# Mixers head by head over both token halves, with the residual stream in DRAM and the output product behind the loop

## The chip, the cores and the metric

The kernel runs on one core of one Trainium2 chip. The metric is the device time of one execution in microseconds (us). Engines are named as in the profile: PE is TensorE (PEld its weight loads), DVE is VectorE, ACT is ScalarE, POOL is GpSimd, SP is SyncE, which here only issues DMAs.

## The reference

The input is x with 1024 tokens of 1024 numbers in float32. Two layers follow each other: layer 0 mixes tokens by gated linear attention (GLA, 4 heads, keys of 128, values of 256), layer 1 by the gated delta rule (GDN, 8 key heads and 16 value heads of 128, with a causal convolution of width 4 in front). Each is followed by a dense feed-forward part (FFN), and a norm ends the whole.

```python
for i in range(DEPTH):
    hn = rms_norm(h, mix_norm_w[i])
    if i % N_MIXERS == 0:
        h = h + gla_mixer(hn, ...)
    else:
        h = h + gdn_mixer(hn, ...)
    h = h + swiglu(rms_norm(h, ffn_norm_w[i]), ffn_w_gate_up[i], ffn_w_down[i])
return rms_norm(h, final_norm_w)
```

Both mixers have the same frame: a projection `hn @ w_in` gives q, k, v, gates and an output gate; a recurrence over the tokens keeps a state per head; its output is normed, multiplied by the SiLU of the output gate, and multiplied by `w_out`, which mixes all heads. The recurrence is computed by chunks of 128 tokens. For GDN each chunk needs the inverse of a triangular matrix (`solve` and `join` in the kernel).

## The kernel before, in words

**Precision.** Operands are split into a high and a low part, and a product takes three matmuls: high x high, low x high, high x low (`mm3`, L151 to L155; these three lines carry nearly all of PE's work). The high part of a weight block is an ACT cast (L122), the low part a POOL subtraction (L123), both in `loadw`, 128x1024 at a time.

**Tokens in halves.** The 1024 tokens are worked on in two halves of 512 columns. The residual stream `h` stays in SBUF all the time (4 MB, `self.h`). A mixer runs through units (half, head): 8 units in GLA, 16 in GDN (a GDN unit is one key head with its two value heads), all heads of half 0 first. So each unit loads and splits its head's weight blocks for its own half only, and each weight block is loaded and split twice in a layer. The states of all heads wait in SBUF (`S_`) for the second half.

**The order.** `pipeline` (L454) writes the steps of several units among each other by a string, in GLA

```python
"seq out-1 decay+1 late+1 prep+1 keys+2 post values+2",
```

and in GDN "solve+1 seq late+1 keys+2 out-1 prep+2 values+2 post join+1". `keys`, `values` and `late` are projections, `prep` builds the matrices of a unit's chunks, `solve` inverts 32x32 blocks on DVE (31 pairs L712, L714 that depend on each other), sends them through DRAM and back (L719, L722), `join` (L729 to L750) joins the blocks, `seq` is the recurrence chunk by chunk, `post` norms and gates its output. A scheduler then orders each engine's instructions; each engine runs its own queue in order.

**Output product.** `gateout` (L258) gates a unit's output and splits it (`ohi`, `olo`, L265, L266). `outproj` (L254) loads the 256 rows of `w_out` that belong to the unit, and `addout` (L231) adds their product to the residual, one DVE addition (L240) for each 128 tokens and 512 columns. This is the step `out-1`: the out-projection of the unit before, inside the loop.

**FFN.** `ffnhead` (L845) norms half 0 and does the first products of the FFN with it; it is the `tail` of the pipeline and stands within the last unit. `inputsums` (L910), at the FFN's start, needs the normed half 1 (L936, L940). The FFN's products use a scheme of seven block products instead of eight; `downs` (L1017) takes its down projection in passes of three or two k-tiles of each half of the rows, reads the activations (`act`) from DRAM, sums blocks (L1045), splits them (L1050, L1051) and adds each product to the residual (L1061).

## Time and profile before

| | before |
|---|---|
| median of 3 runs (lowest to highest) | 3312.35 us (3310.05 to 3316.11) |
| the profiled execution's own time | 3317.64 us |
| its span in the trace | 3315.9 us |
| mean granted clock of PE | 0.958 of full speed |
| busy: PE / DVE / ACT / POOL | 2979.9 / 2174.2 / 1386.2 / 1564.2 us |

In this execution the GLA mixer lasts to about 604 us, FFN 0 to 1283.5, the GDN mixer to about 2626, FFN 1 to about 3300; the final norm ends the span. The shares of busy time are means over these stages. A row of a timeline gives start, duration, engine, line, operation, tiles written and read, and in brackets how long the engine was idle before and what it waited for; x2 means two instructions in one row. Durations of PE overlap, so the rate of matmuls is read from their starts.

### The profile page before, as it was taken

The page shows a single profiled execution, that of the slowest core. Times are in us where ns is not written, and L with a number is a line of the kernel's source. Part 1 is how long each engine was busy: PE and PEld are TensorE (multiplying, and loading weights), DVE is VectorE, ACT ScalarE, POOL GpSimd, SP SyncE. Part 2 cuts the span into 40 slices and gives each one's busy share as a digit, 9 for nine tenths or more (in the row PEclk, how much of TensorE's full clock was granted, in tenths as well). Part 3 has the DMA queues.
Part 4 walks back from the last instruction along what each step waited for, and adds up shares of the span by engine and source line. Part 5 has one row for each costly group of instructions (what it writes and reads, how often), then busy time and mean ns, then how long its engine had stood idle before and what let it go on. Part 6 is the DMA issues. An engine that isn't in the chain of part 4 may idle for free. (4 is left out here: it accounts for less than half of the span.)

```text
span 3315.9 us, 40871 instructions
## 1 busy us (share of the span) xinstructions
PE 2979.9 (90%) x14323; PEld 2422.4 (73%) x14323; DVE 2174.2 (66%) x4493; ACT 1386.2 (42%) x2605; POOL 1564.2 (47%) x1069
## 2 busy tenths in 40 slices
PE   6988989799998999788898988899988889999898
PEld 5877877578886777677676766777776678887676
DVE  6465665633225996768888888888878542232998
ACT  5345444334343334444444544444444433333333
POOL 4344443455556874433333333333432355554885
PEclk9999999899999999899999999999999999999999
DMA  4222212322223312222222222222222232222331
GB/s 127 73 59 58 70 58 78 107 83 83 83 77 121 111 67 53 69 61 59 62 69 63 53 74 63 65 76 68 63 68 60 70 111 81 85 83 82 138 104 58
DMA packets 364924, 256.40 MB, mean 77 GB/s; under 512 B 67847, under 2 KB 309966, under 8 KB 364718
## 3 DMA queue, kind: packets, MB, share of 16 engines
q1 hardware_dynamic: 364654, 253.77, 25.8%
q8 instruction: 113, 1.85, 0.2%
q14 instruction: 93, 0.76, 0.1%
q0 software_dynamic: 64, 0.02, 0.0%
HBM read 219.12 MB, written 34.60 MB: 77 GB/s over the span
## 5 line engine op out<-in xcount | busy, mean ns | idle before, releaser
L123 POOL TENSOR_TENSOR wlo<-raw,whi 128x1024 fp32r<-128x1024 f32 x204 | 490.2, 2405 | 842.7 <-ACT whi L122 716.9
L153 PE MATMUL pd<-xhi,whi 128*128 128x512 f32 x1072 | 442.8, 414 | 0.9 <-ACT xhi L193 0.9
L154 PE MATMUL pd<-xlo,whi 128*128 128x512 f32 x1072 | 437.1, 408 | 0.0
L155 PE MATMUL pd<-xhi,wlo 128*128 128x512 f32 x1072 | 434.0, 405 | 0.0
L122 ACT CAST whi<-raw 128x1024 fp32r<-128x1024 f32 x204 | 214.0, 1049 | 295.0 <-issue 119.2
L895 POOL TENSOR_TENSOR olo<-s,ohi 128x512 fp32r<-128x512 f32 x152 | 195.9, 1290 | 206.1 <-ACT ohi L894 206.1
L895 POOL TENSOR_TENSOR olo<-raw,ohi 128x512 fp32r<-128x512 f32 x138 | 190.3, 1382 | 209.3 <-ACT ohi L894 181.7
L155 PEld LDWEIGHTS pd<-xhi,wlo 128*128 128x128 f32 x1072 | 205.6, 192 | 39.6 <-issue 0.3
L153 PEld LDWEIGHTS pd<-xhi,whi 128*128 128x128 f32 x1072 | 206.2, 193 | 38.7 <-ACT xhi L193 1.4
L154 PEld LDWEIGHTS pd<-xlo,whi 128*128 128x128 f32 x1072 | 206.6, 193 | 37.1
L153 PE MATMUL pd<-whi,ohi 128*128 128x512 f32 x384 | 164.5, 429 | 35.5 <-ACT k L586 22.5
L712 DVE TENSOR_TENSOR tmpx<-nbx,xix 128x60 f32<-128x60 f32 (+24 forms) x496 | 187.1, 377 | 9.9
L894 ACT CAST ohi<-s 128x512 fp32r<-128x512 f32 x152 | 94.3, 622 | 230.9 <-PE pd L154 172.9
L894 ACT CAST ohi<-raw 128x512 fp32r<-128x512 f32 x138 | 85.1, 621 | 197.9 <-POOL olo L895 176.0
L714 DVE TENSOR_TENSOR xix<-xix,tmpx 128x60 f32<-128x60 f32 (+24 forms) x496 | 160.9, 324 | 10.2
L154 PE MATMUL pd<-wlo,ohi 128*128 128x512 f32 x384 | 161.0, 419 | 0.0
L1051 POOL TENSOR_TENSOR blo<-t,bhi 128x1536 fp32r<-128x1536 f32 (+1 forms) x32 | 126.8, 3963 | 69.1 <-ACT bhi L1050 64.2
L155 PE MATMUL pd<-whi,olo 128*128 128x512 f32 x384 | 158.3, 413 | 0.9 <-DVE olo L266 0.9
L240 DVE TENSOR_TENSOR h<-h,pd 128x512 f32<-128x512 f32 x192 | 130.2, 682 | 44.0 <-PE pd L155 42.9
L1003 DVE TENSOR_TENSOR p<-p,pp 128x512 f32<-128x512 f32 x38 | 26.1, 688 | 197.5 <-DMA raw<-in_ffn_w_gate_up_dram 148.3
L153 PE MATMUL pd<-bhi,ahi 128*128 128x512 f32 x264 | 110.6, 419 | 36.7 <-DVE h L1061 21.3
L153 PEld LDWEIGHTS pd<-whi,ohi 128*128 128x128 f32 x384 | 76.0, 198 | 63.6 <-ACT k L586 27.2
(387 smaller groups left out, 8320.2 us busy)
## 6 DMA issues: line engine op xcount, KB each, us to landing
raw<-in_gdn_w_in_dram SPq DMA_DIRECT2D x96, 512.0 KB, 4.0
raw<-in_ffn_w_gate_up_dram SPq DMA_DIRECT2D x176, 256.0 KB, 3.3
raw<-in_gla_w_in_dram SPq DMA_DIRECT2D x48, 512.0 KB, 3.9
ra<-act SPq DMA_DIRECT2D x88, 256.0 KB, 5.1
rb<-in_ffn_w_down_dram SPq DMA_DIRECT2D x24, 768.0 KB, 6.5
raw<-in_gdn_w_out_dram SPq DMA_DIRECT2D x32, 512.0 KB, 4.2
act<-p SPq DMA_DIRECT2D x44, 256.0 KB, 2.0
act<-u SPq DMA_DIRECT2D x38, 256.0 KB, 2.0
```

The source lines that it names most:

```text
L122: nc.scalar.copy(hi, raw)
L123: nc.gpsimd.tensor_tensor(out=lo, in0=raw, in1=hi.bitcast(F32), op=ALU.subtract)
L153: mm(ps, lhs[0], rhs[0], start=first, stop=False, **kw)
L154: mm(ps, lhs[0], rhs[1], start=False, stop=False, **kw)
L155: mm(ps, lhs[1], rhs[0], start=False, stop=last, **kw)
L240: self.nc.vector.tensor_tensor(out=o, in0=o, in1=ps, op=ALU.add)
L712: V.tensor_tensor(out=tv, in0=nbx[:, s, s + 1:].unsqueeze(2).to_broadcast([P, n, w]), in1=xv[:, s:s + 1, 0:w].to_broadcast([P, n, w]), op= ...
L714: V.tensor_tensor(out=xv[:, s + 1:, 0:w], in0=xv[:, s + 1:, 0:w], in1=tv, op=ALU.add)
L894: self.nc.scalar.copy(hi, src)
L895: eng.tensor_tensor(out=lo, in0=src, in1=hi.bitcast(F32), op=ALU.subtract)
L1003: V.tensor_tensor(out=p1, in0=p1, in1=pb, op=ALU.add)
L1051: eng.tensor_tensor(out=lo, in0=src, in1=hi.bitcast(F32), op=ALU.subtract)
```

## The change

**Heads outside, halves inside.** `project` loads a weight block once and yields the product of both halves; the loops go over heads, and a head's state lives only through its two halves (a half of a head is called a half-step below). Each mixer block is so loaded and split once: the program's 128x1024 weight splits fall from 204 to 84 on ACT and on POOL, in GDN from eight to three in a half-step. The buffers of split weights go from three to two. The order is written out as calls in place of `pipeline` and its strings. Both halves are normed before the loop.

**The residual leaves SBUF.** `openh` loads it into a pool on the right side, `closeh` frees that pool behind the norms, and behind the mixer's loop it is loaded again, from x in layer 0 and from a DRAM copy (`spill`) in layer 1.

**The output product.** `gateout` only gates; the result goes to DRAM tiles `act`. Behind the loop `outs` does a direct product with the first four of these tiles, and `downs` takes the rest (four tiles in GLA, twelve in GDN) by the seven-product scheme, two k-tiles a pass (`most`). `ffnhead` follows.

```diff
-        self.h = self.cp.tile([P, KT, D], F32, name="h")
...
+        self.openh(a["x"][0])
...
+    def closeh(self):
+        self.hs.__exit__(None, None, None)
+
+    def weightpools(self, es):
+        self.wr, self.ws, self.tp = (self.pool(es, *x) for x in (("wraw", 2), ("wsplit", 2), ("units", 2)))
+
+    def mixer(self, stage, l, src, w_out):
+
+        with ExitStack() as es:
+            self.xp = self.pool(es, "xmix", 1)
+            self.weightpools(es)
+            act = stage(es)
+        self.openh(src)
...
+        with ExitStack() as es:
+            self.weightpools(es)
+            self.outs(w_out, act[:4])
+            self.downs(w_out[4 * P:], act[4:], 2)
+            self.ffnhead(l)
...
+        for half, x in enumerate(xs):
+            ps = self.dps()
+            self.chan(ps, w, 0, x)
+            yield half, ps
+
+    def gateout(self, pool, ps, w, sz, dst):
+
+        y = pool.tile([P, HT], F32, name="y", tag="y", bufs=2)
+        self.nc.vector.scalar_tensor_tensor(out=y, in0=ps, scalar=w, in1=sz, op0=ALU.mult, op1=ALU.mult)
+        self.nc.sync.dma_start(dst, y)
...
+            for hd in range(4):
+                nxt = hd + 1 < 4
+                if nxt:
+                    keys(hd + 1, U[hd + 1])
+                seq(hd, 0, U[hd][0])
+                if nxt:
+                    decay(hd + 1, U[hd + 1])
+                    prep(hd + 1, 0, U[hd + 1][0])
+                    values(hd + 1, U[hd + 1])
+                seq(hd, 1, U[hd][1])
+                if nxt:
+                    prep(hd + 1, 1, U[hd + 1][1])
+                    late(hd + 1, U[hd + 1])
+        return act
...
+            for hq in range(NQ):
+                solve(hq, 1, U[hq][1])
+                seq(hq, 0, U[hq][0])
+                q_(hq + 1)
+                run(prep, hq + 1, 0)
+                v_(hq + 1)
+                post(hq, 0, U[hq][0])
+                join(U[hq][1])
+                run(solve, hq + 1, 0)
+                seq(hq, 1, U[hq][1])
+                if hq + 1 < NQ:
+                    late(hq + 1, U[hq + 1])
+                k_(hq + 2)
+                run(prep, hq + 1, 1)
+                post(hq, 1, U[hq][1])
+                if hq + 1 < NQ:
+                    join(U[hq + 1][0])
+        return act
...
+    def outs(self, w, act):
...
+            for ch in range(2):
+                r = ar.tile([P, 4, HT], F32, name="rw", tag=f"rw{ch}")
+                nc.sync.dma_start(r, wv[:, 0:4, ch * HT:(ch + 1) * HT])
+                raws.append(r)
+            ws = [self.operand(oo, r, G, "ow") for r in raws]
+            for th in range(2):
+                x = ar.tile([P, 4, HT], F32, name="rx", tag="rx")
+                for i in range(4):
+                    nc.sync.dma_start(x[:, i, :], act[i][:, th * HT:(th + 1) * HT])
+                x = self.operand(oo, x, G, "ox")
+                for ch in range(2):
+                    for t in range(C):
+                        ps = self.dps()
+                        self.prod(ps, [v[:, :, t * P:(t + 1) * P] for v in x], ws[ch])
+                        o = self.hh[th][:, t, ch * HT:(ch + 1) * HT]
+                        V.tensor_tensor(out=o, in0=o, in1=ps, op=ALU.add)
...
-                kp = 3 if (n - at) % 3 == 0 else (n - at) % 3
...
+                kp = (n - at) % most or most
...
+        k.mixer(k.gla, 0, a["x"][0], a["gla_w_out"][0])
+        k.ffn(0)
+        k.mixer(k.gdn, 1, k.spill(), a["gdn_w_out"][0])
+        k.ffn(1)
```

**Where the order moves.** The rows below are the order of an engine's queue, before and after, with each kernel's own line numbers (L177 to L179 after the change are L153 to L155 before).

PE at the end of GLA, before: the last head's transposes (L440) of the normed output `on` stand between out-projection, the FFN head's norm transposes (L210) and the head's products.

```order
L153 MATMUL pd<-whi,ohi 128x512
L154 MATMUL pd<-wlo,ohi 128x512
L155 MATMUL pd<-whi,olo 128x512
L210 MATMUL pp<-cst,xn 128x128 x8
L440 MATMUL pq<-cst,on 128x128 x7
L153 MATMUL pd<-xhi,whi 128x512 x2
L440 MATMUL pq<-cst,on 128x128
L210 MATMUL pp<-cst,xn 128x128 x4
L154 MATMUL pd<-xlo,whi 128x512
L155 MATMUL pd<-xhi,wlo 128x512
L210 MATMUL pp<-cst,xn 128x128 x4
```

PE at the end of GLA, after the change: the end of the first half's recurrence of the last head (L424 to L427, `st`, `kt` and `qg` its prepared matrices), its transposes (L441), and the beginning of the second half's.

```order
L425 MATMUL pq<-v,st 128x256
L427 MATMUL pq<-v,kt 128x256
L441 MATMUL pq<-cst,on 128x128 x8
L424 MATMUL pq<-state,qg 128x256
L425 MATMUL pq<-v,st 128x256
L427 MATMUL pq<-v,kt 128x256
```

No projection stands between the two, and none among their chunks. The second recurrence goes on so to its end, where the output product (`ow`, `ox`) begins:

```order
L427 MATMUL pq<-v,kt 128x256
L424 MATMUL pq<-state,qg 128x256
L425 MATMUL pq<-v,st 128x256
L441 MATMUL pq<-cst,on 128x128 x8
L177 MATMUL pd<-owhi,oxhi 128x512
L178 MATMUL pd<-owlo,oxhi 128x512
```

Nothing else is left on PE between the recurrences and the output product.

ACT at the same place: squares and normed outputs of the last recurrence, the casts of the output weight (`rw`) and of the first activations (`rx`), and the first of `downs`.

```order
L435 ACTIVATE sq,ss<-pq 128x256
L437 ACTIVATE on<-pq,rs_y 128x256
L435 ACTIVATE sq,ss<-pq 128x256
L437 ACTIVATE on<-pq,rs_y 128x256 x2
L895 CAST owhi<-rw 128x2048 x2
L895 CAST oxhi<-rx 128x2048 x2
L1076 CAST bhi<-rb 128x1024
L1076 CAST ahi<-ra 128x1024
```

POOL has the low parts in the same order, `owlo` twice and then `oxlo` twice. The casts have moved behind the last recurrence's ACT work.

PE at the end of GDN, before: the FFN head's products (into `pp`) stand around the last unit's transposes (L825), and the last out-projection follows.

```order
L154 MATMUL pp<-xlo,whi 128x512
L155 MATMUL pp<-xhi,wlo 128x512
L825 MATMUL pq<-cst,o 128x128 x6
L153 MATMUL pp<-xhi,whi 128x512
L154 MATMUL pp<-xlo,whi 128x512
L155 MATMUL pp<-xhi,wlo 128x512
L153 MATMUL pp<-xhi,whi 128x512
```

PE at the end of GDN, after the change: the last chunk of the second half's recurrence, its transposes (L796), and the output product at once.

```order
L738 MATMUL pq<-gstate,k 128x256
L739 MATMUL pq<-gstate,q 128x256
L754 MATMUL pq<-rt,tt 128x128 x2
L774 MATMUL pq<-un,at 128x128 x2
L796 MATMUL pq<-cst,o 128x128 x8
L177 MATMUL pd<-owhi,oxhi 128x512
L178 MATMUL pd<-owlo,oxhi 128x512
L177 MATMUL pd<-owhi,oxhi 128x512
L178 MATMUL pd<-owlo,oxhi 128x512
L179 MATMUL pd<-owhi,oxlo 128x512
```

The head's products, which stood among the last recurrence's, have moved behind the output product.

## Rows read from the trace of the kernel before

**Rows 1.** page, part 1: busy us, share and instructions of each engine

```profile
PE 2979.9 (90%) x14323; PEld 2422.4 (73%) x14323; DVE 2174.2 (66%) x4493; ACT 1386.2 (42%) x2605; POOL 1564.2 (47%) x1069
```

**Rows 2.** windows, GDN: start:end length, busy us (instructions) PE PEld DVE ACT POOL

```profile
1398.86:1676.37 277.51, 238.19 (x1235) 195.01 (x1236) 213.13 (x600) 124.76 (x296) 95.02 (x108) 0.94 0.25 64
...
1470.34:2565.95 1095.61, 968.97 (x4929) 772.89 (x4927) 895.50 (x2380) 493.55 (x1150) 391.42 (x383) 0.95 0.25 65
```

**Rows 3.** timeline of PE, dense out-projection, the first and last of 24

```profile
2553.82 0.40 PE L153 MATMUL pd<-whi,ohi 128*128 128x512 f32 x1
...
2559.19 0.39 PE L155 MATMUL pd<-whi,olo 128*128 128x512 f32 x1
```

**Rows 4.** page, part 5: the costliest groups of instructions

```profile
L123 POOL TENSOR_TENSOR wlo<-raw,whi 128x1024 fp32r<-128x1024 f32 x204 | 490.2, 2405 | 842.7 <-ACT whi L122 716.9
...
L122 ACT CAST whi<-raw 128x1024 fp32r<-128x1024 f32 x204 | 214.0, 1049 | 295.0 <-issue 119.2
...
L153 PE MATMUL pd<-whi,ohi 128*128 128x512 f32 x384 | 164.5, 429 | 35.5 <-ACT k L586 22.5
...
L240 DVE TENSOR_TENSOR h<-h,pd 128x512 f32<-128x512 f32 x192 | 130.2, 682 | 44.0 <-PE pd L155 42.9
```

**Rows 5.** lines L712 and L588 and tile wlo: ns min/median/max

```profile
L712 DVE TENSOR_TENSOR tmpx<-nbx,xix x440: 158/234/2511, 1453.0 to 2549.0; 128x60 f32<-128x60 f32 x14, 128x48 f32<-128x48 f32 x10, 128x54 f32<-128x54 f32 x10, 128x28 f32<-128x28 f32 x10
...
L588 DVE SCALAR_TENSOR_TENSOR v<-raw,col_conv,v x78: 733/752/2833, 1534.3 to 2498.2; 128x512 f32<-128x512 f32 x78
...
L123 POOL TENSOR_TENSOR wlo<-raw,whi x109: 2339/2390/3027, 1473.4 to 2561.8; 128x1024 fp32r<-128x1024 f32 x109
```

**Rows 6.** timelines of DVE and ACT in GLA's last unit

```profile
538.91 0.48 DVE L426 SCALAR_TENSOR_TENSOR state<-state,eg,pq 128x256 f32<-128x256 f32 x1
...
541.15 0.48 DVE L426 SCALAR_TENSOR_TENSOR state<-state,eg,pq 128x256 f32<-128x256 f32 x1
...
551.38 0.47 ACT L432 ACTIVATE on<-pq,rs_y 128x256 f32<-128x256 f32 x1 [1.24 <-DVE rs_y L182]
```

**Rows 7.** windows of the start, the GLA loop and GDN's end

```profile
0.00:50.00 50.00, 33.16 (x185) 26.58 (x186) 31.26 (x67) 26.50 (x43) 19.02 (x15) 1.00 0.58 182
...
100.00:550.00 450.00, 414.85 (x2318) 350.56 (x2317) 275.08 (x702) 203.80 (x365) 188.53 (x103) 0.98 0.22 63
...
2560.00:2613.00 53.00, 51.92 (x288) 41.93 (x286) 25.16 (x54) 27.79 (x67) 18.73 (x10) 1.00 0.28 88
```

**Rows 8.** timeline of PE: start of each FFN's sums

```profile
611.10 1.97 PE L940 MATMUL pp<-cst,xn 128*128 128x128 f32 x8 [9.80 <-DVE xn L936]
...
2634.90 1.97 PE L940 MATMUL pp<-cst,xn 128*128 128x128 f32 x8 [8.83 <-DVE xn L936]
```

**Rows 9.** join's transposes in GDN; DVE and ACT timelines of its last unit

```profile
L729 DVE STREAM_TRANSPOSE xd<-xt x16: 1231/1238/1246, 1398.9 to 2565.9; 128x1024 f32<-128x1024 f32 x16
...
2575.25 0.61 DVE L771 SCALAR_TENSOR_TENSOR rt<-pq,neg,vt 128x128 f32<-128x128 f32 x2 [0.65 <-PE pq L767]
...
2594.20 0.29 ACT L813 ACTIVATE osq<-o 128x128 f32<-128x128 f32 x1
```

**Rows 10.** timelines: DVE, recurrence and solve; SP and DVE, a trip through DRAM

```profile
2037.79 0.61 DVE L771 SCALAR_TENSOR_TENSOR rt<-pq,neg,vt 128x128 f32<-128x128 f32 x2 [0.65 <-PE pq L767]
...
2071.03 0.17 DVE L714 TENSOR_TENSOR xix<-xix,tmpx 128x8 f32<-128x8 f32 x1
...
1390.43 2.62 SPq L719 DMA_DIRECT2D d<-xix  x4
...
1398.86 1.25 DVE L729 STREAM_TRANSPOSE xd<-xt 128x1024 f32<-128x1024 f32 x1 [8.46 <-DMA xt<-d]
```

**Rows 11.** DVE's first additions of two passes; the window of the first pass

```profile
1045.83 0.69 DVE L1061 TENSOR_TENSOR h<-h,pd 128x512 f32<-128x512 f32 x1 [2.17 <-PE pd L155]
...
1086.41 1.27 DVE L1061 TENSOR_TENSOR h<-h,pd 128x512 f32<-128x512 f32 x2
...
1045.00:1089.00 44.00, 37.46 (x148) 29.36 (x148) 39.29 (x34) 17.35 (x16) 41.53 (x13) 0.93 0.49 174
```

More of the change, by code (lines that the diff above doesn't have):

```diff
@@ new lines, in late, with decay @@
+            def late(hd, U):
+                for half in range(2):
+                    U[half]["r"] = self.tp.tile([P, 2, HT], F32, name="r", tag="sz", bufs=3)
+                for i in range(2):
+                    for half, ps in self.project(w_in, 2048 + hd * 256 + i * P, xs):
+                        S.activation(U[half]["r"][:, i, :], ps, AF.Silu)
+            def decay(hd, U):
+                e = mx.tile([P, 2, HT], F32, name="e", tag="e")
+                g2 = mx.tile([P, 2, HT], F32, name="g", tag="g")
+                b = self.bgate[:, hd:hd + 1]
+                for j in range(2):
+                    ps = self.prepps()
+                    TE.matmul(ps, wgu[:, hd * P:(hd + 1) * P], glow[j], start=True, stop=True)
+                    S.activation(e[:, j], ps, AF.Abs, bias=b)
+                    V.tensor_scalar(out=g2[:, j], in0=ps, scalar1=b, scalar2=0.0, op0=ALU.add, op1=ALU.min)
+                S.activation(e, e, AF.Exp, scale=-1.0)
+                S.activation(e, e, AF.Ln, bias=1.0)
+                V.tensor_tensor(out=e, in0=g2, in1=e, op=ALU.subtract)
+                for j in range(2):
+                    V.tensor_tensor_scan(out=g2[:, j], data0=reset, data1=e[:, j], initial=0.0, op0=ALU.mult,
+                                         op1=ALU.add)
+                    U[j]["g"] = g2[:, j]
@@ L499, in gdn @@
-    def gdn(self, tail):
+                    self.gateout(mx, ps, self.glaw[:, dt:dt + 1], u["r"][:, dt, :],
+                                 act[2 * hd + dt][:, half * HT:(half + 1) * HT])
+            U = [[{}, {}] for _ in range(4)]
+            keys(0, U[0])
+            first()
+            decay(0, U[0])
+            prep(0, 0, U[0][0])
+            values(0, U[0])
+            prep(0, 1, U[0][1])
+            late(0, U[0])
+            for hd in range(4):
[11 more added lines that the diff above has]
+                    late(hd + 1, U[hd + 1])
@@ L602, in late @@
[L602 to L603 removed]
+                last = None
+                for half, ps in self.project(w_in, ct * P, xs):
+                    U[half][nm] = out = self.tp.tile([P, HT], F32, name=nm, tag=nm[0], bufs=4)
+                    raw = mx.tile([P, HT + 3], F32, name="raw", tag="raw", bufs=2)
+                    S.copy(raw[:, 3:], ps)
+                    if half == 0:
+                        G.memset(raw[:, 0:3], 0.0)
+                        last = raw
+                    else:
+                        G.tensor_copy(raw[:, 0:3], last[:, HT:HT + 3])
+                    S.activation(out, ps, AF.Copy, scale=tap(3))
+                    for s in range(3):
+                        V.scalar_tensor_tensor(out=out, in0=raw[:, s:s + HT], scalar=tap(s), in1=out,
+                                               op0=ALU.mult, op1=ALU.add)
+                    S.activation(out, out, AF.Silu)
@@ L723, in solve, with join @@
                 r.update(kt=kt, vt=vt)
-            def join(half, hq, r):
+            def join(r):
                 nt = r["nt"]
@@ L825, in post @@
                         TE.transpose(ps[:, c * P:(c + 1) * P], o[:, c, h2, :], self.ident)
-                    oT.append(self.gateout(mx, h2, ps, self.gdnw, sz[:, h2, :]))
-                return oT
-            self.pipeline(
-                [(half, hq) for half in range(2) for hq in range(NQ)],
-                "solve+1 seq late+1 keys+2 out-1 prep+2 values+2 post join+1",
-                norm=lambda half: self.normx(half, self.mixw[1], self.xp, *((mx, "raw") if half else (self.tp, "vch"))),
-                gates=gates, proj=proj, late=late, prep=prep, solve=solve, join=join, seq=seq,
-                post=lambda o, u: post(o, u["z"]),
-                wout=lambda half, hq, oT: self.outproj(half, w_out, hq * 256, oT), tail=tail)
+                    self.gateout(mx, ps, self.gdnw, u["z"][:, h2, :],
+                                 act[2 * hq + h2][:, half * HT:(half + 1) * HT])
@@ new lines, in gdn, with v_ @@
+            U = [[{}, {}] for _ in range(NQ)]
+            k_ = lambda hq: hq < NQ and conv(8 + hq, "k", U[hq])
+            q_ = lambda hq: hq < NQ and conv(hq, "q", U[hq])
+            def v_(hq):
+                if hq < NQ:
+                    conv(16 + 2 * hq, "v0", U[hq])
+                    conv(17 + 2 * hq, "v1", U[hq])
+            run = lambda f, hq, half: hq < NQ and f(hq, half, U[hq][half])
+            k_(0)
+            gt = gates()
+            q_(0)
+            prep(0, 0, U[0][0])
@@ new lines, in gdn @@
+            v_(0)
+            solve(0, 0, U[0][0])
+            join(U[0][0])
+            prep(0, 1, U[0][1])
+            k_(1)
+            late(0, U[0])
+            for hq in range(NQ):
[15 more added lines that the diff above has]
+                    join(U[hq + 1][0])
```

381 lines of the change are left out of this document (137 added, 244 removed).

## The prediction

> **What bounds the kernel now.** I read the page first: TensorE is busy 2979.9 of 3315.9 us, 90%, far ahead of every other engine [rows 1]. So the time is the matmuls plus some 336 us in which TensorE has nothing, and the change has to be priced as matmuls removed and idle time added or filled, stage by stage. The windows say where the idle time is. Over 14 steady units of the GDN mixer (from one join's transposes to those 14 units later) a unit takes 1095.61 / 14 = 78.3 us and TensorE is busy 968.97 / 14 = 69.2 of it, VectorE 895.50 / 14 = 64.0; idle are 9.1 [rows 2]. The first four units, which hold on average 168 large matmuls where a steady one holds 192, take 277.51 / 4 = 69.4 us with 59.5 busy [rows 2]. Where matmuls have what they need, one of 512 columns starts every (2559.19 - 2553.82) / 23 = 0.2335 us [rows 3].
>
> **Matmuls.** The out-projection inside the loop was 1152 matmuls (its three products have 384 each [rows 4]). Behind the loops stand instead 384 direct ones and 672 of the seven-product scheme: 96 fewer, 24 in GLA and 72 in GDN, -5.6 and -16.8 us at 0.2335 (GDN's share is inside the comparison of whole stretches below). Everything else of the change moves work or adds waits.
>
> **GDN, half-step by half-step.** The new loop has 16 half-steps; 14 of them are whole. Each holds 144 large matmuls on average (alternately 137 and 151) where a unit held 192, so TensorE's share falls from 69.2 to 69.2 - 48 x 0.2335 = 58.0 us. VectorE loses eight h additions of 0.68 us [rows 4] and two olo splits of about the same size, 64.0 - 6.8 = 57.2.
>
> It also loses a hindrance. The solve's small L712 takes 234 ns in the middle, but 2511 at worst, and the convolution's L588 0.752 us in the middle and 2.833 at worst; these worst cases are as long as a weight split on POOL, 2.39 us [rows 5]. Splits per half-step fall from eight to three, since one serves both halves. Each split removed may give VectorE anything from nothing to 2.39 us back; I take 1 us, so 5 us, and VectorE comes to 52.
>
> [...]
>
> What is left is the balance within a pair of half-steps. VectorE's order has, between two joins, alternately 194 instructions (three convolutions of both halves, two preparations) and 109. I put the heavy one's VectorE work at 52 + 10 = 62 and the light one's at 42, an estimate from these counts. The heavy half-step is then bound by VectorE, 62 plus 5 of waits = 67; the light one by TensorE, 151 matmuls, 58.0 + 7 x 0.2335 = 59.6 plus 1.4 = 61. Mean 64. The rows bracket this: the first four units less their 24 surplus matmuls give 69.4 - 5.6 = 63.8, and a steady unit less 48 gives 78.3 - 11.2 = 67.1. I take 64, near the lower, because there is less on VectorE and POOL than in either.
>
> Then the tail, which has no projections left to fill it. Before, the first join's transposes begin at 1398.9, the last ones at 2565.9, and the FFN's sums can start at 2634.90: together 1236.0 us [rows 8, 9]. After, I count from the same first join to the same place:
> 14 half-steps of 64 = 896;
> a bare one: 9.3 from the join's transposes to the recurrence (2565.9 to 2575.25 [rows 9]), 33.4 for the recurrence with the solve woven in (2037.79 to 2071.2), 8.4 for the solve's trip through DRAM (1390.43 to 1398.86 [rows 10]) = 51.1;
> the last join and recurrence, bare, 2565.9 to 2594.5 = 28.6 [rows 9];
> the start of the output product: its casts stand on ACT behind the last recurrence's squares, and the third matmul of a group needs the low part of both operands. That is one cast of 128x2048 and three splits on POOL in series. Such sizes are not in the trace; twice the 128x1024 ones, 2 x 1.05 + 3 x 2 x 2.40 = 16.5 [rows 4]. Lower bound 5, if the first splits are done early, upper 22;
> 192 direct matmuls = 44.8;
> three seven-product passes of two k-tiles. The one pass of this size before takes 40.6 from its first addition to the next pass's first (1045.83 to 1086.41 [rows 11]): 121.8;
> the FFN's head: 144 matmuls, which before filled the last recurrence (51.92 busy of 53 us there [rows 7]) = 33.6, plus 4 for its norm. Half 0 of the residual is final two products before the end, so most of the norm chain hides under those 48 matmuls.
> Sum 896 + 51.1 + 28.6 + 16.5 + 44.8 + 121.8 + 37.6 = 1196.4. The entry is later by the second half's norm and gates, which stood inside the loop: 10, between 0 and the 16.8 us that TensorE idles in the kernel's first 50 [rows 7]. So 1206.4 against 1236.0: **-29.6**. The wait of 8.83 us before the FFN's sums [rows 8] is within this comparison: half 1's residual is now final before the head, so that it is covered.
>
> **GLA.** The matmuls, -5.6. The start: half 1's x is loaded and normed ahead of the first weights, +6 (0 to 16.8, as above). The loop: TensorE idles 35 of 450 us there [rows 7]; fewer splits may take 8 of it, and the value weights, whose two blocks now fill both buffers, so that no next block can be split ahead, may add 8: 0, each side a bound. The tail: both recurrences of the last head end without projections. Four chunks follow each other at 2.24 us, and from the first state update to the end of the last normalised output are 12.9 [rows 6]; the second half's cannot start before the first's 9.0: 22. Then the output product's start, 16.5 as above: 38.5, in which TensorE still does the two recurrences' own products and transposes, which I put at 10: +28. If that part is hidden better, +15; with waits for the loads, +38. The norm ahead of the FFN's head, +3. The wait of 9.80 us for half 1's residual [rows 8] goes, with about 1 of slow clock behind it: -10.8. Sum **+20.6**.
>
> **What costs nothing.** The spill of the residual (eight transfers of 512 KB out, 16 back in two layers) stands on the DMA queues while the mixer runs, and the reload must be there only for the first addition of the output product; behind the last recurrence it has the 16.5 us of the splits. If it came late it would add up to some 10 us in each layer. On SP the loads of the output weight and of the first four activation tiles stand ahead of the last head's stores, so they don't wait for it. The activation tiles' trip through DRAM is needed only by the passes behind the direct part, 44.8 us later.
>
> **Sum.** -29.6 + 20.6 = -9.0. The profiled execution took 3317.64 us, so 3308.6; it stands 5.3 above the runs' median of 3312.35, hence 3303.3, a little faster (-0.3%).
>
> **TensorE's clock.** [...] A mean of 0.93 over 44 us is worth 3 us, which the 40.6 of the pass already holds, so I add nothing. [...]
>
> **Rivals.**
> *More than forecast (0.20).* Each of POOL's splits holds VectorE up for its whole length, and the loss of five gives 5 x 2.39 = 12 us in a half-step, not 5. The heavy half-step falls to 61, TensorE-bound, the mean to 61: 14 x 3 = 42 less, 3261. For it: the worst cases in rows 5. Against: POOL also makes the decay's tables, and these stay. It decides where a half-step is below 62.
> *Slower: VectorE binds the loop (0.25).* The heavy half-steps' 194 instructions don't overlap with their neighbours', since the join, the recurrence and the next solve form one chain on VectorE and the out-projection, which could fill any gap, is gone. At 67.5 a half-step, which is 67.1 and a little for the imbalance: 14 x 3.5 = +49, 3352. The sum turns from a gain to a loss at 64.6. For it: the steady rows scaled, 67.1; against: the first four units.
> *Nothing to see or slightly slower (0.15).* The loop does what I say, but both tails wait some 8 to 15 us longer, for reloads and stores on SP: 3320.
> *The forecast (0.40)*: 3285 to 3322 by a half-step between 63 and 65 and tails within 5.
>
> **Range and chances.** 3258 takes in the first rival, 3355 the second. A measurement of this kernel tells about 0.2%, 6.6 us, from no change. Faster: the first rival and 0.65 of the forecast, 0.46; same: 0.25 of the forecast and a third of the neutral case, 0.15; slower: 0.39.
>
> **What would show it.** Join transposes 67 and 61 us apart in turn, with TensorE busy 58 us of each; some 90 us of nearly idle TensorE ahead of the GDN output product and some 38 ahead of GLA's; POOL's 128x2048 splits at about 4.8 us each as what the third product waits for; passes of 40.6; no wait of 9 us before the FFN's sums. I am wrong if the half-steps lie outside 63 to 65, if the tails hold work that I missed (the reload, the stores), or if the GLA loop stalls on its two weight buffers.

## The result, and the profile after

The change makes the kernel slower: 3415.56 us median (3409.39 to 3423.46, four runs) against 3314.23 us for the kernel before (3310.05 to 3322.17, four runs), a ratio of 1.0304 with a 95% interval of 1.0275 to 1.0334. The prediction was 3303 with a range from 3258 to 3355. The profiled execution took 3423.46 us with a span of 3421.7, 105.8 more than before (the medians differ by 101.3); the mean granted clock is 0.936 against 0.958.

The span is cut at five places that both kernels have: the FFN's first product with a block sum `t1` (FFN 0 and FFN 1), the last product of FFN 0, and the first and the last of the sixteen join transposes in GDN.

| us | GLA | FFN 0 | GDN entry | first to last join | last join to FFN 1 | FFN 1 and end |
|---|---|---|---|---|---|---|
| before | 614.6 | 668.8 | 115.4 | 1167.1 | 72.8 | 677.1 |
| after | 658.9 | 664.0 | 142.3 | 977.8 | 298.0 | 680.7 |
| difference | +44.3 | -4.8 | +26.9 | -189.3 | +225.2 | +3.6 |
| forecast | +20.6 | 0 | +10 | -220 | +180 | 0 |

The loop did get shorter, by 189. What was put behind it costs 225, and GLA and the entry of GDN each lose what the prediction gave them and more. (The forecast's cells are its own terms: for the loop 896 + 51.1, for the tail the rest of its sum and the 3.9 from the FFN's sums to its first `t1` product.)

From the page of after, part 1 and one group of part 5 (the solve's small products, L712 before):

```profile
PE 2989.5 (87%) x14223; PEld 2438.5 (71%) x14223; DVE 2089.3 (61%) x4411; ACT 1315.9 (38%) x2497; POOL 1448.5 (42%) x967
...
L681 DVE TENSOR_TENSOR tmpx<-nbx,xix 128x60 f32<-128x60 f32 (+24 forms) x496 | 146.0, 294 | 9.0
```

TensorE has 100 matmul records fewer than in [rows 1] and is still busy 9.6 us longer, at a lower mean clock. But its busy time grew far less than the span: 432 us of the span are now without it, where 336 were. The windows show where:

```profile
494.00:504.50 10.50, 2.44 (x4) 1.12 (x4) 0.00 (x0) 0.57 (x1) 10.49 (x3) 0.50 0.95 380
504.50:549.00 44.50, 44.41 (x188) 36.32 (x188) 10.33 (x16) 3.20 (x3) 4.61 (x1) 0.96 0.35 119
549.00:601.00 52.00, 43.35 (x168) 34.45 (x169) 47.10 (x61) 16.62 (x23) 34.92 (x12) 0.90 0.00 1
...
2061.57:2117.07 55.50, 51.59 (x274) 42.79 (x274) 36.91 (x114) 23.04 (x66) 9.38 (x13) 0.94 0.19 47
2117.07:2194.86 77.79, 64.05 (x336) 52.30 (x336) 66.28 (x200) 39.77 (x87) 25.75 (x31) 0.93 0.17 46
...
2382.50:2443.00 60.50, 29.56 (x132) 22.83 (x132) 28.61 (x115) 14.92 (x47) 5.81 (x6) 0.61 0.31 81
2443.00:2496.50 53.50, 27.73 (x130) 22.01 (x130) 18.61 (x43) 18.10 (x48) 13.47 (x3) 0.66 0.17 58
...
2542.00:2682.00 140.00, 122.48 (x505) 95.82 (x506) 132.47 (x139) 44.18 (x51) 95.19 (x34) 0.98 0.20 64
2682.00:2741.00 59.00, 44.24 (x194) 33.34 (x192) 30.66 (x44) 21.57 (x35) 28.55 (x18) 0.93 0.23 76
...
2682.00:2702.30 20.30, 11.40 (x57) 7.72 (x55) 19.82 (x28) 9.22 (x18) 17.77 (x13) 0.92 0.22 65
```

The columns are those of [rows 2]; behind POOL stand the granted clock, the busy share of the DMA engines and GB/s. The first three rows are GLA behind its loop: the wait for the output product's operands, the direct product, one seven-product pass. The next two are one light and one heavy half-step in the middle of GDN. Then comes GDN's end: the bare half-step, the last join and recurrence with the wait, the three passes, the head, and the head's first 20 us by themselves. Read four things. The half-steps take 55.5 and 77.8 in turn, where the forecast had 61 and 67. In the bare stretches the clock is 0.61 and 0.66, and TensorE is busy half of the time. In the three passes VectorE is busy 132.47 of 140.00 us, TensorE 122.48: VectorE is the fuller engine. And the head takes 59 where its matmuls need 33.6; in its first 20.30 us VectorE is busy 19.82, with the norms, and TensorE 11.40.

The waits themselves, in the timelines of ACT and PE, and in the lists of PE's waits (us in total, times, longest), the last row from the kernel before:

```profile
1322.70 1.04 ACT L142 CAST whi<-raw 128x1024 fp32r<-128x1024 f32 x1 [15.36 <-PE pp L178]
...
1333.34 0.90 PE L234 MATMUL pp<-cst,xn 128*128 128x128 f32 x3 [10.50 <-DVE xn L231]
...
2496.53 0.80 PE L179 MATMUL pd<-owhi,oxlo 128*128 128x512 f32 x1 [8.53 <-POOL oxlo L896]
```

```profile
PE pq L706 <- DVE xd L698: 60.7, 10, 16.5
...
PE pd L179 <- POOL oxlo L896: 15.8, 2, 8.5
...
PE pq L737 <- DVE xd L729: 18.0, 3, 8.2
```

The first two rows are the entry of GDN: a weight cast that stands idle on ACT, and TensorE's wait for the first norm. The third is the forecast wait for POOL's splits, which comes in both layers (15.8 us together). The join's wait for the transposed inverse, 60.7 us in ten places, was 18.0 in three places before.

### The profile page after: what moved, and what is told of

The parts are those of the page before. It is cut to its first block, busy times and chain, and to the rows that moved or that the text cites. A ratio compares the mean times of both kernels' runs of the same rounds, so it can differ in the third digit from the quotient of the medians.

```text
span 3421.7 us, 40258 instructions
## 1 busy us (share of the span) xinstructions
PE 2989.5 (87%) x14223; PEld 2438.5 (71%) x14223; DVE 2089.3 (61%) x4411; ACT 1315.9 (38%) x2497; POOL 1448.5 (42%) x967
## 5 line engine op out<-in xcount | busy, mean ns | idle before, releaser
L177 PE MATMUL pd<-xhi,whi 128*128 128x512 f32 x1072 | 442.6, 413 | 0.0
L179 PE MATMUL pd<-xhi,wlo 128*128 128x512 f32 x1072 | 438.4, 409 | 3.8 <-POOL wlo L143 3.8
L143 POOL TENSOR_TENSOR wlo<-raw,whi 128x1024 fp32r<-128x1024 f32 x84 | 205.1, 2445 | 537.6 <-ACT whi L142 455.5
L179 PEld LDWEIGHTS pd<-xhi,wlo 128*128 128x128 f32 x1072 | 206.6, 193 | 43.7 <-POOL wlo L143 5.7
L177 PEld LDWEIGHTS pd<-xhi,whi 128*128 128x128 f32 x1072 | 207.4, 194 | 38.0 <-ACT xhi L217 0.9
L1077 POOL TENSOR_TENSOR blo<-t,bhi 128x1024 fp32r<-128x1024 f32 (+1 forms) x48 | 168.8, 3517 | 95.8 <-ACT bhi L1076 86.2
L177 PE MATMUL pd<-bhi,ahi 128*128 128x512 f32 x360 | 149.5, 415 | 45.0 <-DVE h L1087 26.4
L1077 POOL TENSOR_TENSOR blo<-rb,bhi 128x1024 fp32r<-128x1024 f32 (+1 forms) x36 | 131.3, 3647 | 109.8 <-PE pd L179 62.3
L681 DVE TENSOR_TENSOR tmpx<-nbx,xix 128x60 f32<-128x60 f32 (+24 forms) x496 | 146.0, 294 | 9.0
L142 ACT CAST whi<-raw 128x1024 fp32r<-128x1024 f32 x84 | 88.2, 1050 | 163.3 <-PE pd L178 96.3
L178 PE MATMUL pd<-blo,ahi 128*128 128x512 f32 x360 | 146.8, 408 | 2.5 <-POOL blo L1077 2.5
L179 PE MATMUL pd<-bhi,alo 128*128 128x512 f32 x360 | 146.7, 408 | 1.5 <-DVE alo L1077 1.4
L1077 DVE TENSOR_TENSOR alo<-s,ahi 128x1024 fp32r<-128x1024 f32 (+1 forms) x48 | 145.2, 3025 | 1.5 <-ACT ahi L1076 1.5
L1076 ACT CAST ahi<-s 128x1024 fp32r<-128x1024 f32 (+1 forms) x48 | 60.7, 1265 | 191.3 <-PE pp L178 121.9
```

Of the source, the lines that this page charges most:

```text
L142: nc.scalar.copy(hi, raw)
L143: nc.gpsimd.tensor_tensor(out=lo, in0=raw, in1=hi.bitcast(F32), op=ALU.subtract)
L177: mm(ps, lhs[0], rhs[0], start=first, stop=False, **kw)
L178: mm(ps, lhs[0], rhs[1], start=False, stop=False, **kw)
L179: mm(ps, lhs[1], rhs[0], start=False, stop=last, **kw)
L681: V.tensor_tensor(out=tv, in0=nbx[:, s, s + 1:].unsqueeze(2).to_broadcast([P, n, w]), in1=xv[:, s:s + 1, 0:w].to_broadcast([P, n, w]), op= ...
```

## Experiments

**Output product without the seven-product scheme.** The first kernel replaces the passes by direct groups of two k-tiles, the second the whole product.

```diff
-            self.downs(w_out[4 * P:], act[4:], 2)
+            self.direct(w_out[4 * P:], act[4:])
```

```diff
-            self.outs(w_out, act[:4])
-            self.direct(w_out[4 * P:], act[4:])
+            self.direct(w_out, act)
```

> The changed kernel with the seven-product passes of the output product replaced by direct products of two k-tiles at a time: 96 matmuls more. My theory: these short passes don't run at TensorE's rate (GDN's three take 139.6 us for 504 matmuls, GLA's one 51.5 us for 168, against 117.7 and 39.2 at 0.2335 us each), because they need more block sums, splits and additions on VectorE and POOL; the direct form takes 576 x 0.2335 = 134.5 and 192 x 0.2335 = 44.8, so 10 to 12 us less: about 3404 us. Rival: TensorE's matmuls set the time here too, 96 x 0.2335 = 22 us more: about 3438 us.

> As e1, and the first part of the output product too in blocks of two k-tiles: the operands that the first product needs are split at half the size, first weight and first activations first. My theory: the wait from the last recurrence to the first full product (19.5 us in GDN, 18.5 in GLA) is the chain of one 128x2048 cast and three such splits, and with one 128x1024 cast and two splits it falls to 6 or 8: 20 to 24 us less than e1 in the two layers, about 3382 us. Rival: the wait is for the loads of the activations or for the memory that the mixer frees, not for the splits: same time as e1.

Measured: 3408.85 us, ratio 1.0293 [1.0270, 1.0316], and 3362.50, 1.0148 [1.0125, 1.0171]. The first adds 96 matmuls, 22 us at 0.2335, and the median is 6.7 lower, too little to tell from no change, since the intervals of the two ratios overlap, but far from 22 more. The window of its direct product in GDN behind the first four tiles:

```profile
2532.40:2668.80 136.40, 134.14 (x577) 110.23 (x578) 71.90 (x122) 30.04 (x41) 61.47 (x28) 0.97 0.28 89
```

577 matmuls in 136.40 us are 0.236 each, with VectorE at 71.90: TensorE's rate. The passes had 72 fewer in GDN and took 140. So a pass isn't priced by its matmuls: in the pass that the forecast's 40.6 comes from, VectorE and POOL were already as full as TensorE [rows 11], and neither GLA's single pass (51.5) nor GDN's three (46.6 each) repeats it.

The second kernel is 46 us faster than the first, where 20 to 24 were expected. GLA gains 16.8, the tail 20.3, and the bare half-step, whose work is the same, 9.1. The window of the bare half-step:

```profile
2356.10:2406.90 50.80, 22.55 (x132) 18.16 (x132) 28.44 (x114) 14.82 (x46) 5.89 (x6) 0.77 0.32 84
```

The same 132 matmuls are busy 22.55 us at a clock of 0.77 and 29.56 at 0.61, and the half-step is 50.8 or 60.5 long. VectorE has the same work in both, 28.4 and 28.6. The product begins with splits half as large, so its third matmul comes 41.8 us behind the last join's transposes (2406.9 to 2448.65), and 53.6 in the change (2442.96 to 2496.53).

**Both kernels without any output product.** One leaves the two lines above out, the other takes `out-1` out of both strings.

```diff
-                "solve+1 seq late+1 keys+2 out-1 prep+2 values+2 post join+1",
+                "solve+1 seq late+1 keys+2 prep+2 values+2 post join+1",
```

> The changed kernel without any output product (the gated outputs are stored, but neither multiplied nor added; the residual passes the mixers unchanged). The product's stages and their start chains last 20 + 45 + 140 us in GDN and 19 + 44 + 51 in GLA: about 319 us less, 3097 us. To be read beside e4. My theory (about half of the loss comes from what both halves' ending together leaves bare: the last recurrences, the FFN's head, the norms; half from the product behind the loop): e3 is 40 to 60 us above e4. Rival 1 (the new order of the loop loses everything): about 100 above. Rival 2 (only the product's new place loses): no more than 10 above.

> The kernel before without the output product in its loops (the outputs are gated and split, but neither multiplied nor added). If the product's 1152 matmuls are on the path throughout, 269 us less: 3045 us. If they fill time in which TensorE would wait anyway, less: I expect 220 to 250 us less, 3065 to 3095 us, which is then the price of the product in the loop, against some 319 behind it.

Measured: 3126.19 us, 0.9437 [0.9416, 0.9457], and 3118.00, 0.9412 [0.9392, 0.9432]. Here are the windows from the first to the last join, first the kernel by heads, then the kernel before, both without the product:

```profile
1371.00:2346.30 975.30, 823.49 (x4363) 675.87 (x4363) 735.69 (x2285) 444.02 (x1098) 242.97 (x302) 0.92 0.17 46
```

```profile
1319.50:2382.50 1063.00, 876.72 (x4578) 709.86 (x4579) 825.02 (x2419) 535.45 (x1233) 361.77 (x383) 0.92 0.23 58
```

This pair carries most of the argument. The order by heads alone costs 8.2 us by the medians, where 40 to 60 had been expected. In the profiled executions it costs 14.0: its loop is 87.7 shorter (65.0 us a half-step in the mean against 70.9 a unit), and entries and tails eat that up (GLA +28.9, entry +31.1, tail +52.4, FFNs -10.6). The output product costs 195 us in the loop of before (6% of 3314) and 289 us behind the loop. Its 1152 matmuls alone are 269 at the dense rate, so in the loop some 74 us of them stood in time that is lost anyway. So some 94 of the loss are the product's place and form, 8 the order. The second kernel of the experiment before parts the 94: with the product in direct groups it takes 3362.50, so that form costs 236 behind the loop. 53 are then the form and the start of the product, 41 its place. Two limits of this account: the kernel before without the product still gates and splits its outputs on ACT and VectorE, and without the product nothing fills either loop, so the 8.2 is the order's price only in that state.

**The head alone moved.** The kernel before, with the FFN's head issued behind the last out-projection instead of in the last unit.

```diff
             if i == len(units) - 1:
-                tail()
...
+        tail()
```

> The kernel before with the FFN's head behind the last out-projection instead of within the last unit. It takes the filler from the last recurrence (22 of its 28.6 us) and gives back the wait before the FFN's sums (9 us in each layer). My theory, that the FFN's head is part of what the order by heads can no longer hide: 12 to 20 us a layer, 24 to 40 in all, about 3345 us. Rival (the head's place does not matter, because its matmuls are on the path anyway): within 10 us of the kernel before.

Measured: 3333.77 us, 1.0059 [1.0040, 1.0077], 17 above the median of the kernel before in the same series (20 by the ratio), where 24 to 40 were expected. In the trace the tail goes from 72.8 to 92.3, GDN's loop gets 4.5 shorter and GLA 2.6 longer. The two heads have 288 matmuls, 67 us at 0.2335.

**The entry.** The weight pools are opened behind both norms, so that no weight buffer can lie in the way of the norm; in a second kernel only the pools of split weights and units are, and the raw blocks keep their place.

```diff
-            self.weightpools(es)
...
             self.closeh()
+            self.weightpools(es)
```

```diff
-            self.weightpools(es)
+            self.ew, self.wr = es, self.pool(es, "wraw", 2)
...
+            self.ws, self.tp = self.pool(self.ew, "wsplit", 2), self.pool(self.ew, "units", 2)
```

> The changed kernel with the pools of the mixer's weights opened behind the norms of both halves. In the changed kernel the first weight cast of GDN stands ahead of the norm's squares on ACT and waits until the last FFN product has read the memory that it overwrites; TensorE then waits 10.5 us for the norm. If that order of the queue is the cause: 8 to 12 us less, about 3405 us. Rival (the norm waits for its own memory or for the residual's last additions): no change.

> The changed kernel with that same edit alone, in both layers. If the cast's place in ACT's queue holds up the norm: the 10.5 us wait ahead of GDN's norm goes and the entry falls from 142 to about 131 us: about 3403 us. If the norm waits for the memory or the residual: no change.

Measured: 3442.29 us, 1.0387 [1.0366, 1.0407], and 3440.97, 1.0379 [1.0364, 1.0394], 25 to 27 slower than the change, where 10 less were hoped for. The entry is 152.7 and 153.7 instead of 142.3, and GLA is some 10 longer in both. In the first the norm's squares run on ACT from 1312.56 on, under the FFN's last products, and TensorE begins the norm's transposes at 1333.11, right behind the FFN's last matmul at 1332.88: the wait of 10.5 is gone. But the first weight block is only loaded from 1362.0 on, and the first projection starts at 1367.18. In the second ACT's first square shows what it waits for (timeline of ACT):

```profile
1332.20 0.63 ACT L247 ACTIVATE jk<-h 128x512 f32<-128x512 f32 x1 [21.67 <-PE pp L178]
```

ACT stands idle for 21.67 us until a product of the FFN is done, with no weight cast ahead of the square in its queue. The square doesn't use that product's operands, so the likely reason is that its buffer lies where they lay; the edit moved that buffer too. So the second kernel says little about the change. There a weight cast stands ahead of the squares on ACT and is idle for 15.36 us (the row at 1322.70), and the first kernel, without it, loses the norm's wait. So the trace of the change and this kernel both put the 10.5 down to the cast's place in ACT's queue, and taking it away cost more than it gave.

**The product within the last recurrences.** The residual is reloaded into the normed tokens' buffers, which are free by then, and the direct product is issued in groups of two k-tiles: in one kernel the first groups (two in GLA, three in GDN) stand among the last recurrences, in the other all stand behind the loop.

```diff
                 seq(hq, 0, U[hq][0])
+                if hq + 1 == NQ:
+                    self.openx()
+                    for _ in range(1):
+                        self.group(act)
...
                 seq(hq, 1, U[hq][1])
+                for _ in range(1 if hq + 1 == NQ else 0):
+                    self.group(act)
```

> As e7b, but two groups in GLA and three in GDN are issued within the last head's recurrences, where the changed kernel has nothing for TensorE: their first act tiles are long in DRAM. Theory (the product costs more behind the loop because it no longer fills time in which TensorE waits, and because the bare stretch lowers the granted clock): five groups of 22.4 us move into idle time, less 20 to 40 for additions and splits that now stand among the recurrences' own VectorE work: 70 to 90 us less than e7b, about 3280, and the granted clock of the last 120 us of GDN's loop back above 0.9. Rival (the last recurrences are bound by VectorE, so that work put there lengthens them as much): within 20 us of e7b.

> Control for the next run. The changed kernel with the output product in direct groups of two k-tiles (96 matmuls a group, four groups in GLA, eight in GDN), all behind the loop; the residual is loaded into the buffers that the normed tokens leave behind the last projection. Same work as e2 by other buffers: 3350 to 3375 us by either theory.

Measured: 3337.11 us, 1.0070 [1.0052, 1.0088], and 3336.82, 1.0062 [1.0040, 1.0083]: equal. The second was no control. With no pool in the way the scheduler puts its groups among the last recurrences too, as the windows of the last half-step show (first the kernel with the groups there, then the other):

```profile
2371.20:2445.00 73.80, 64.91 (x321) 51.63 (x321) 54.44 (x145) 20.55 (x53) 22.79 (x13) 0.95 0.33 97
```

```profile
2370.80:2442.10 71.30, 61.63 (x320) 48.96 (x321) 54.22 (x146) 21.75 (x54) 22.70 (x13) 1.00 0.34 100
```

Both hold 321 and 320 matmuls where the change had 132, at a clock of 0.95 and 1.00. Against the whole direct product behind the loop the tail falls from 270 to 213, the loop grows by 29 and GLA by 8: 25 gained, about a third of the 70 to 90 that were expected. The buffers differ too, so not even the 25 belong to the groups' place alone.

**Balance of heavy and light half-steps.** One of the two output-gate projections is moved from the light to the heavy half-step, once in the change and once in the kernel with the groups.

```diff
                 solve(hq, 1, U[hq][1])
+                if hq:
+                    late(hq, U[hq], (1,))
...
-                    late(hq + 1, U[hq + 1])
+                    late(hq + 1, U[hq + 1], (0,))
```

> The changed kernel with one of the two output-gate projections of a head (48 matmuls, no VectorE work) moved from the light half-step, which takes 54.5 us with TensorE busy 51.5, to the heavy one, which takes 77.8 with TensorE busy 64.0 and VectorE 66. Theory (the light half-step is bound by TensorE, and the heavy one has 13 us of room on it): light to about 45, heavy up by 1 to 4, so 6 to 8 us for each of seven pairs, 40 to 56 in all, about 3368 us. Rival (the heavy half-step is a chain in which TensorE's queue waits in order, and what is added to it lengthens it as much): no change.

> The two edits that helped or should, together: the direct output product issued within the last recurrences (as in e7) and the output-gate projection moved to the heavy half-step (as in e8). If e8's theory holds: 3337 less 40 to 50, about 3292 us, below the kernel before. If it does not: 3337.

Measured: 3424.29 us, 1.0340 [1.0324, 1.0355], and 3353.16, 1.0125 [1.0110, 1.0140], so 9 and 16 slower than without it. Windows of a pair of half-steps in the first:

```profile
1931.16:1996.68 65.52, 54.83 (x279) 44.42 (x279) 48.57 (x153) 28.50 (x72) 14.27 (x19) 0.86 0.18 47
1996.68:2064.31 67.63, 60.48 (x333) 49.25 (x331) 52.06 (x160) 34.46 (x80) 19.69 (x25) 0.98 0.18 46
```

The half-steps are even now, 65.5 and 67.6, but the pair takes 133.1, against 55.50 + 77.79 = 133.3 above. The expected 6 to 8 us a pair did not come. VectorE's 48.57 and 52.06 are far from full, and TensorE is busy 115 of the 133 us as before. So the pair's length isn't VectorE's work in the heavy half-step plus TensorE's in the light one.

**Useless matmuls.** The change, with 72 and 120 matmuls without a use among the last recurrences of GLA and GDN.

```diff
+                if hq + 1 == NQ:
+                    self.warm(xs, 5)
```

> The changed kernel with 72 matmuls in GLA and 120 in GDN added among the last head's recurrences, on the normed tokens, into PSUM that nothing reads: work that is of no use, 45 us of it at 0.2335. Theory (the bare stretches are long because TensorE's granted clock falls to 0.61 there and doubles the recurrences' own small matmuls): the last interval of joins falls from 60.5 to 51 to 55 us, and the whole is 10 to 20 us faster than the changed kernel, about 3400 us. Rival (the chain on VectorE and ACT sets these stretches, whatever the clock): the added matmuls cost nothing or up to 20 us.

Measured: 3413.55 us, 1.0310 [1.0292, 1.0327]: 2 us under the change, which is within the noise. The window of the bare half-step:

```profile
2380.20:2438.00 57.80, 39.69 (x231) 32.37 (x229) 32.08 (x114) 14.96 (x46) 5.86 (x6) 0.87 0.30 84
```

The clock is 0.87 instead of 0.61, and the half-step is 2.7 shorter although 99 matmuls were added. Expected were a half-step of 51 to 55 and 10 to 20 us in all. The timeline of PE shows why so little came of it. The recurrence itself became 7.9 us shorter: from the join's first product to the third `gstate` product it takes 22.3 us (2386.34 to 2408.59), in the change 30.2 (2383.80 to 2413.95). But 27 of the useless matmuls stand ahead of that first product in TensorE's queue, and it starts 6.1 us behind the join's transposes instead of 1.3.

**GLA as before, GDN as in the kernel with the groups.** The second kernel adds the second form of the entry above.

```diff
-        k.mixer(k.gla, 0, a["x"][0], a["gla_w_out"][0])
+        k.gla(tail=lambda: k.ffnhead(0))
```

> GLA as in the kernel before (halves outside, output product and FFN head inside the loop), GDN by heads with the output product issued within the last recurrences, as in e7. If the stages are separate: GLA 614.6 and FFN 0 at about 667 from the kernel before, GDN's entry, loop and tail 1349.6 from e7 against 1355.3 before: 3305 to 3315 us, no change to be told from the kernel before. If GLA's new order also paid for something later: above 3325.

> e11, with the weight loads' pool opened ahead of the norms and the pools of split weights and units behind them, so that the first weights are loaded early and no cast stands ahead of the norm's squares on ACT. If GDN's entry waits for that cast: 8 to 15 us less than e11, about 3298 us, just below the kernel before. If not: as e11.

Measured: 3310.65 us (11 runs against 17 of before, 3313.05), 0.9989 [0.9980, 0.9999], and 3322.53, 1.0030 [1.0019, 1.0040]. The first stands within 0.2% of the kernel before; its stages (GLA 614.7, loop 993.8, tail 214.0) are those of the two kernels that it is made of. The second is 12 us slower, where 8 to 15 less were hoped for; its entry is 154.0. The best form of the order by heads that was found gives GDN as much as it takes.

## Why the prediction was wrong

The sum was -9.0 and the trace says +105.8. The 114.8 between them, by the prediction's own terms: GDN's tail 44.8, GLA 23.7, the half-steps 21.3, the entry 16.9, the bare half-step 9.4, and -1.2 in the FFNs.

**The tail: priced as matmuls, and TensorE isn't what sets its pace.** This is the step that failed. Of the 44.8, the three passes are 17.9 (139.7 instead of 121.8): VectorE fills them, and direct groups with 72 more matmuls take 136.4. The head is 17.4 (58.9 instead of 37.6 and the 3.9 to the first `t1` product). Its term "plus 4 for its norm" is the one that was mis-sized: in the first 20.30 us VectorE is busy 19.82, with the norm of half 0 and the beginning of that of half 1, and only 57 of the head's 194 products and transposes run there. Before, the head's 33.6 us of matmuls filled the last recurrence's waits; behind everything, nothing fills its own waits. The head's move alone cost the kernel before 19.5 in GDN's tail (15 with the shorter loop), less than the head's matmuls. The last join and recurrence are 5.4 longer, the start of the product 3.1, the direct product 1.2. The mechanism of the start was right, POOL's splits hold the third product: 19.6 from the last square to it, forecast 16.5. POOL's three splits are 4.5 each, and in GDN it stands idle for 3.97 us between the first two, until a VectorE instruction of the last head (L266) is done; that wait was not in the sum. The third rival put 8 to 15 on both tails together, for reloads and stores; the waits that end last in these rows are not theirs.

**GLA.** Forecast +20.6, measured +44.3, from the same kind: the product starts 43.2 behind the last projection (38.5 forecast), its pass takes 51.5 where its matmuls are 39.2, its head 57.7 where I had 36.6 and the 3.5 to the first `t1` product. The two recurrences alone take 27.9 instead of 22: in the first the chunks' `state` products start 2.1 us apart (462.85 to 464.98), in the second 3.5 (475.63 to 479.13), and the same matmul takes 1.06 us there instead of 0.59. The rest of GLA was about 10 better than forecast.

**The loop: nearly right in size by two errors that cancel.** "A steady unit less 48 matmuls gives 78.3 - 11.2" took each removed matmul as 0.2335. The kernel before without its out-projection has units of 70.9 in the mean instead of 77.8: the 48 matmuls, with the loads, splits and additions that went with them, are worth 6.9, less than the 11.2 of the matmuls alone. So part of the out-projection stood in TensorE's waits. The order by heads with shared weights then gave 5.9 more, to 65.0, where the prediction had about 3. VectorE's part of that came out as forecast, 36.91 and 66.28 in a pair are 51.6 a half-step against 52, but partly by luck. Of the 57.2 - 51.6 = 5.6 us, some 2.8 are work that the steady units of before held and the new half-steps don't: the norm and the gates of half 1 and the norm of the FFN's head (an estimate, summed by line over the 14 units of [rows 2]). That leaves about 3, some 0.6 for each of the five splits that went, where the forecast had 1 and the first rival the full 2.39. The solve's L681 shows the relief in its mean, 294 ns against 377 for L712 before. Of the 496 L681, eleven take 2.02 to 2.50 us; each of them began while a weight split (L143, some 2.4 us) ran on POOL and ended 0.03 to 0.14 us behind that split's end, the longest from 1513.69 to 1516.19 under a split from 1513.58 to 1516.05. The longest L712 before was the same case (1510.17 to 1512.68, the split 1510.12 to 1512.53). So these instructions were held up nearly for a whole split, as the first rival has it, but on average a removed split gave back far less than its length.

What bounds a half-step was wrong. "The heavy half-step is bound by VectorE, the light one by TensorE" would have made moving a projection a gain; even half-steps take as long as uneven ones. Nor is the imbalance the one forecast: 77.8 and 55.5 instead of 67 and 61. The second rival (VectorE binds the loop, 67.5) named the right kind, a chain that nothing fills, yet its half-step was too long and its place wrong. Which chain sets the 133 us of a pair stays open; the join's 60.7 us of waiting for the inverse may speak for the solve and its way through DRAM, but that is not shown: no experiment has taken it away.

**The clock: "I add nothing".** The bare half-step is 60.5 instead of 51.1. At a clock of 0.77 it takes 50.8, as forecast, and at 0.61 60.5, with the same matmuls: a term of about 9.5 that the prediction left out. The same product of the recurrence in the change and in the second kernel of the first experiment:

```profile
2406.72 1.19 PE L738 MATMUL pq<-gstate,k 128*128 128x256 f32 x2 [0.36 <-DVE gstate L768]
...
2375.48 0.67 PE L737 MATMUL pq<-gstate,k 128*128 128x256 f32 x2 [0.57 <-DVE gstate L767]
```

It comes once in a chunk, and each chunk needs the state of the one before: in the change these products start 7.15 and 7.23 us apart, in the other kernel 5.10 and 5.19. In the kernel with the useless matmuls they are 5.09 and 5.26 apart, so there the chain had its speed back, and most of the gain was lost in the queue ahead of the join. Whether the same filler behind the join would win was not tried. A lower clock behind a wait was in the trace of before: 0.66 from 611 to 621 us and 0.65 from 2635 to 2645, behind TensorE's waits of 9.80 and 8.83 [rows 8], and 1.00 in the 20 us after each; in the change both waits are gone, and it is 1.00 from 650 to 680, but 0.70 from 2741 to 2751. The size in the bare half-step is three times the 3 us that the prediction took from 0.93 over a pass, since the slow matmuls form a chain. Why the second kernel had 0.77 was not settled.

**The entry.** 10 was forecast, 26.9 it is. The first norm waits 10.5, because a weight cast stands ahead of its squares on ACT and is itself held until the FFN's last products are done. The other 16, the second half's norm among them, were not separated. The attempt that took the wait away moved the loading of the weights behind both norms, and the other put a wait of 21.67 us on the norm itself.

**What was right:** the count of matmuls (100 records fewer, 96 forecast) and their rate where they are dense, the place of the waits behind both loops, and that the reload of the residual costs little: while it runs (380 GB/s in the row at 494 us), the wait that ends last is POOL's. The wait of 9 us ahead of the FFN's sums is gone as forecast.

## What to carry to other kernels

Before you price work that is moved out of a loop by the engine's rate, ask what it filled there: leave it out of both kernels, and the difference is its price in each place, here 195 us in the loop, 269 as bare matmuls, and behind it 289 in the form chosen, 236 in direct groups. The loop that ends both halves of the work together has a tail here that nothing fills (114 us in GDN, with TensorE busy 57 of them), and any filler for it must have been kept back. The dense stages here took the time of their fullest engine, which is read from the windows: VectorE with the block sums in the passes (132.47 of 140.00 us) and with a norm at the head's start (19.82 of 20.30), TensorE in the direct product (134.14 of 136.40).

## What the runs showed of the hardware

The granted clock of a stretch with few matmuls differed between kernels whose work in it is the same, and went with its length: 60.5 us at 0.61, 61.2 at 0.56 (the first kernel of the entry), 53.0 at 0.76 (the first with even half-steps), 50.8 at 0.77. At 0.61 a chunk of GDN's recurrence took 7.15 and 7.23 us, at 0.77 (the second kernel of the first experiment) 5.10 and 5.19. The 192 useless matmuls, 45 us at the dense rate, cost no measurable time in sum: some of them delayed the join by about 5 us, and the recurrence behind them ran 7.9 us faster, in a half-step at a clock of 0.87. The out-projection in the loop of before cost 195 us, three quarters of what its matmuls alone take at the dense rate.
